# Row normalisation streamed through one core: one hardware DMA queue in a fixed order of load runs and store runs, in place of two queues mixed packet by packet

## The chip, the cores and the metric

The kernel runs on 1 core of one Trainium2 chip. The metric is the device time of one execution in microseconds (us). DVE is the vector engine and ACT the scalar engine, which compute here; SP is the sync engine, which only issues transfers. HBM is the chip's memory, SBUF the buffer in the core. A transfer runs as *packets* on 16 DMA engines. "L" is a load (HBM to SBUF), "S" is a store (SBUF to HBM), and a *turn* is the place in a queue where a load is followed by a store.

## The reference

```python
def reference(x):                      # x: float32 [32, 512, 1024]
    sums = np.sum(np.abs(x), axis=-1, keepdims=True)
    return (x / (sums + 1e-8)).astype(np.float32)
```

67.1 MB are read and 67.1 MB are written, each once; every row of 1024 values is divided by its own sum.

## The kernel before

The 16384 rows are 128 partitions x 128 rows. They are cut into 11 tiles: ten of 12 rows per partition (6 MB each) and one of 8 rows (4 MB), in 4 buffers that take turns. The loads are issued from the sync engine (SP) and the stores from ACT, so they are on two DMA queues.

```python
    R = 12
    BUFS = 4
    ...
    sbuf = ctx.enter_context(tc.tile_pool(name="sbuf", bufs=BUFS))
    ...
    def normalize(x_tile, r0, k, kv):   # DVE: sum of |x|, +eps, 1/x; then
        ...                             # rows 0..kv-1 scaled on DVE, the rest on ACT

    with tc.manual_schedule():
        for i, k in enumerate(rows):
            x_tile = sbuf.tile([P, R, d], FP32)
            nc.sync.dma_start(out=x_tile[:, :k, :], in_=piece(x_flat, i))
            normalize(x_tile, 0, k, k // 2)
            nc.scalar.dma_start(out=piece(out_flat, i), in_=x_tile[:, :k, :])
```

A load into a buffer waits until the store out of that buffer has landed. That wait is on the issuing sequencer (SP), not in the queue.

Of the kernel before, what the change touches and what calls it, by code (L numbers as in the profile page):

```python
# [1 line left out]

# [4 lines left out]

FP32 = mybir.dt.float32
EPS = 1e-8


@with_exitstack
def kernel(
    ctx: ExitStack,
    tc: tile.TileContext,
    x: bass.AP,
    out: bass.AP,
):
    nc = tc.nc
    P = nc.NUM_PARTITIONS  # L20

    x_flat = x.flatten_outer_dims()
    out_flat = out.flatten_outer_dims()
    n, d = x_flat.shape


    R = 12
    BUFS = 4
    per_partition = n // P
    assert n % P == 0  # L30
    rows = [R] * (per_partition // R)
    if per_partition % R:
        rows.append(per_partition % R)

    def piece(flat, i):
        a, k = P * sum(rows[:i]), rows[i]
        return flat[a : a + P * k, :].rearrange("(p r) d -> p r d", p=P)

    sbuf = ctx.enter_context(tc.tile_pool(name="sbuf", bufs=BUFS))
    stats = ctx.enter_context(tc.tile_pool(name="stats", bufs=4))  # L40

    def normalize(x_tile, r0, k, kv):

        s = stats.tile([P, R], FP32)
        nc.vector.tensor_reduce(  # L45
            out=s[:, :k],
            in_=x_tile[:, r0 : r0 + k, :],
            axis=mybir.AxisListType.X,
            op=mybir.AluOpType.add,
            apply_absolute_value=True,  # L50
        )
        nc.vector.tensor_scalar_add(out=s[:, :k], in0=s[:, :k], scalar1=EPS)  # L52
        inv = stats.tile([P, R], FP32)
        nc.vector.reciprocal(out=inv[:, :k], in_=s[:, :k])  # L54
        nc.vector.tensor_mul(  # L55
            out=x_tile[:, r0 : r0 + kv, :],
            in0=x_tile[:, r0 : r0 + kv, :],
            in1=inv[:, :kv].unsqueeze(2).to_broadcast([P, kv, d]),
        )
        for r in range(kv, k):  # L60
            row = x_tile[:, r0 + r, :]
            nc.scalar.activation(  # L62
                out=row,
                in_=row,
                func=mybir.ActivationFunctionType.Copy,
                scale=inv[:, r : r + 1],
            )

    with tc.manual_schedule():
        for i, k in enumerate(rows):  # L70
            x_tile = sbuf.tile([P, R, d], FP32)
            nc.sync.dma_start(out=x_tile[:, :k, :], in_=piece(x_flat, i))  # L72
            normalize(x_tile, 0, k, k // 2)
            nc.scalar.dma_start(out=piece(out_flat, i), in_=x_tile[:, :k, :])  # L74


# [1 line left out]
_INS = ['x']  # L78
_OUTS = [((32, 512, 1024), 'float32')]


# [23 lines left out]
```

## Time and profile before

| | before |
|---|---|
| median of 4 runs | 317.66 us (317.55 to 318.85) |
| span of the profiled run | 315.8 us |
| DVE, ACT busy | 67%, 22% |
| packets on the 16 DMA engines | 98.9% of the span |

Lines of the profile page of the kernel before. The rows of digits are busy tenths in 40 equal slices of the span. The last two lines give packets, MB and the share of the 16 DMA engines' span for each queue.

```profile
span 315.8 us, 227 instructions
DVE 212.4 (67%) x44; ACT 69.0 (22%) x65; POOL 0.2 (0%) x4
DVE  0069999998499079719944991797099449949300
ACT  0010804308007000700440070007003400701300
DMA  8999999999999999999999999999999999999996
GB/s 311 467 417 411 467 367 442 405 454 430 417 448 430 423 461 423 436 442 417 442 442 411 449 436 411 448 436 423 448 430 436 442 413 450 421 448 417 448 403 278
q1 hardware_dynamic: 1584, 67.11, 49.8%
q10 hardware_dynamic: 1584, 67.11, 49.1%
```

The DMA row stands at 9 from the second slice to the last but one, and the two queues (q1 loads, q10 stores) together hold 98.9% of the engines' time. DVE has gaps in every period. So the DMA engines are the limit, and a change can help only by moving the same bytes faster or by shortening the two ends.

Stretches of the same execution, from the windows view: a load-only stretch, two periods of mixed loads and stores, and the store-only end. The last two columns are the DMA share and GB/s.

```profile
core 0: us, DVE busy (x) ACT busy (x) POOL busy (x), PEclk, DMA share, GB/s
20.00:38.00 18.00, 17.90 (x4) 6.19 (x6) 0.00 (x0) 1.00 1.01 437
103.00:132.00 29.00, 19.91 (x5) 6.34 (x7) 0.00 (x0) 1.00 1.00 434
132.00:161.00 29.00, 19.90 (x5) 6.34 (x7) 0.00 (x0) 1.00 1.00 434
285.00:300.00 15.00, 9.92 (x4) 4.27 (x4) 0.00 (x0) 1.00 1.03 446
```

Packets are large (48 KB, 1.8 us), so a stretch of 15 or 18 us can catch a wave of packet starts more or less; the 29 us stretches are one full period and exact. The packet records say it more finely: a 48 KB packet takes 1.815 us in all three stages. 16 x 49152 B / 1.815 us = 433.3 GB/s. This is close to the 435 GB/s that the Trainium skill gives as the ceiling of the 16 ports ("DMA: Bandwidth & Descriptors", section "Where 436 GB/s comes from").

What SP waited for, from the waits view of the DMA queues' own engine (us in total, times, longest):

```profile
SPq L72 <- DMA out_dram<-x_tile: 226.5, 7, 55.2
SPq L72 <- DMA x_tile<-in_x_dram: 15.4, 1, 15.4
```

The seven later loads wait for stores to land; this wait costs nothing as long as the queues still hold work.

### The profile page before, as it was taken

To read this page: it belongs to the slowest core of one execution; us is meant where nothing else is said; L and a number is where in the kernel's file an instruction comes from. 1 tells how busy PE (TensorE), PEld (TensorE's weight loads), DVE (VectorE), ACT (ScalarE), POOL (GpSimd) and SP (SyncE) were. 2 spreads that over 40 slices of the span, in tenths; PEclk is the share of its full clock that TensorE was granted. 3 is DMA by queue.
4 is the path that set the end of the run, shared out by engine and by line. 5 is a ranking of instruction groups with operands and counts; after the bars stand their busy time and mean duration, and the time that the engine had idled before them with its cause. 6 is when DMAs were issued, how large, how long until landed. Compare 5 with 4: busy or idle time off the path is not lost.

```text
span 315.8 us, 227 instructions
## 1 busy us (share of the span) xinstructions
DVE 212.4 (67%) x44; ACT 69.0 (22%) x65; POOL 0.2 (0%) x4
## 2 busy tenths in 40 slices
DVE  0069999998499079719944991797099449949300
ACT  0010804308007000700440070007003400701300
POOL 0000000000000000000000000000000000000000
DMA  8999999999999999999999999999999999999996
GB/s 311 467 417 411 467 367 442 405 454 430 417 448 430 423 461 423 436 442 417 442 442 411 449 436 411 448 436 423 448 430 436 442 413 450 421 448 417 448 403 278
DMA packets 3169, 134.23 MB, mean 425 GB/s; under 512 B 352, under 2 KB 352, under 8 KB 352
## 3 DMA queue, kind: packets, MB, share of 16 engines
q1 hardware_dynamic: 1584, 67.11, 49.8%
q10 hardware_dynamic: 1584, 67.11, 49.1%
q14 instruction: 1, 0.01, 0.0%
HBM read 67.11 MB, written 67.11 MB: 425 GB/s over the span
## 4 chain that ended last, share of the span: by engine, by line
DMA 55%; DVE 25%; another core or an unknown queue 9%; ACT 4%; issue 0%; SPq 0%; DVEq 0%; ACTq 0%
DMA x_tile<-in_x_dram 41%; DVE s L45 19%; DMA out_dram<-x_tile 14%; DVE x_tile L55 6%; ACT x_tile L62 4%; DVE inv L54 0%; DVE s L52 0%; SPq L72 0%; DVEq L54 0%; ACTq L74 0%
## 5 line engine op out<-in xcount | busy, mean ns | idle before, releaser
L45 DVE TENSOR_REDUCE s<-x_tile 128x12 f32<-128x12288 f32 (+1 forms) x11 | 138.2, 12564 | 81.1 <-DMA x_tile<-in_x_dram 81.1
L62 ACT ACTIVATE x_tile<-x_tile,inv 128x1024 f32<-128x1024 f32 x64 | 67.7, 1135 | 207.6 <-DVE inv L54 207.6
L55 DVE TENSOR_TENSOR x_tile<-x_tile,inv 128x6144 f32<-128x6144 f32 (+1 forms) x11 | 70.0, 6364 | 0.4
L62 ACT ACT_TABLE_LOAD x1 | 1.3, 1283 | 18.4 <-DMA x_tile<-in_x_dram 18.4
L54 DVE RECIPROCAL inv<-s 128x12 f32<-128x12 f32 (+1 forms) x11 | 2.5, 226 | 0.9
L52 DVE TENSOR_SCALAR s<-s 128x12 f32<-128x12 f32 (+1 forms) x11 | 1.9, 173 | 0.4
L89 POOL MEMSET const-bfloat16-1.0<- 128x1 bf16 x1 | 0.1, 101 | 0.0
L89 POOL MEMSET const-uint8-127<- 128x1 uint8 x1 | 0.1, 101 | 0.0
L89 POOL MEMSET const-float32-0.0<- 128x1 f32 x1 | 0.1, 98 | 0.2 <-issue 0.2
L89 POOL MEMSET const-float32-1.0<- 128x1 f32 x1 | 0.1, 98 | 0.0
## 6 DMA issues: line engine op xcount, KB each, us to landing
x_tile<-in_x_dram SPq DMA_DIRECT2D x10, 6144.0 KB, 38.5
out_dram<-x_tile ACTq DMA_DIRECT2D x10, 6144.0 KB, 53.5
x_tile<-in_x_dram SPq DMA_DIRECT2D x1, 4096.0 KB, 33.7
out_dram<-x_tile ACTq DMA_DIRECT2D x1, 4096.0 KB, 19.5
```

What stands on the lines that cost most here:

```text
L45: nc.vector.tensor_reduce(out=s[:, :k], in_=x_tile[:, r0 : r0 + k, :], axis=mybir.AxisListType.X, op=mybir.AluOpType.add, apply_absolute_v ...
L52: nc.vector.tensor_scalar_add(out=s[:, :k], in0=s[:, :k], scalar1=EPS)
L54: nc.vector.reciprocal(out=inv[:, :k], in_=s[:, :k])
L55: nc.vector.tensor_mul(out=x_tile[:, r0 : r0 + kv, :], in0=x_tile[:, r0 : r0 + kv, :], in1=inv[:, :kv].unsqueeze(2).to_broadcast([P, kv, d]),)
L62: nc.scalar.activation(out=row, in_=row, func=mybir.ActivationFunctionType.Copy, scale=inv[:, r : r + 1],)
L89: nc = _bacc.Bacc("TRN2", target_bir_lowering=False, num_devices=1)
```

## The change

The intent: take the arbitration away from the hardware. All transfers go into one queue, in a fixed order of longer runs in one direction, so that the engines do not alternate between reading and writing HBM at every packet. Four turns from loads to stores are left (L4 S2, L2 S3, L3 S2, L2 S4).

```diff
+    tiles = {}
+
+    def load(i):
+        k = rows[i]
+        x_tile = sbuf.tile([P, R, d], FP32)
+        tiles[i] = x_tile
+        nc.sync.dma_start(out=x_tile[:, :k, :], in_=piece(x_flat, i))
+        normalize(x_tile, 0, k, k // 2)
+
+    def store(i):
+        nc.sync.dma_start(out=piece(out_flat, i), in_=tiles[i][:, : rows[i], :])
+
+    runs = [("L", 4), ("S", 2), ("L", 2), ("S", 3), ("L", 3), ("S", 2), ("L", 2), ("S", 4)]
     # (two asserts on the totals cut)
     with tc.manual_schedule():
-        for i, k in enumerate(rows):
-            x_tile = sbuf.tile([P, R, d], FP32)
-            nc.sync.dma_start(out=x_tile[:, :k, :], in_=piece(x_flat, i))
-            normalize(x_tile, 0, k, k // 2)
-            nc.scalar.dma_start(out=piece(out_flat, i), in_=x_tile[:, :k, :])
+        done = {"L": 0, "S": 0}
+        for what, m in runs:
+            for _ in range(m):
+                (load if what == "L" else store)(done[what])
+                done[what] += 1
```

More of the change, by code (lines that the diff above doesn't have):

```diff
@@ L67, in normalize @@
             )
-    with tc.manual_schedule():
-        for i, k in enumerate(rows):
-            x_tile = sbuf.tile([P, R, d], FP32)
-            nc.sync.dma_start(out=x_tile[:, :k, :], in_=piece(x_flat, i))
-            normalize(x_tile, 0, k, k // 2)
-            nc.scalar.dma_start(out=piece(out_flat, i), in_=x_tile[:, :k, :])
+    tiles = {}
[8 more added lines that the diff above has]
+    runs = [("L", 4), ("S", 2), ("L", 2), ("S", 3), ("L", 3), ("S", 2), ("L", 2), ("S", 4)]
+    assert sum(m for w, m in runs if w == "L") == len(rows)
+    assert sum(m for w, m in runs if w == "S") == len(rows)
+    with tc.manual_schedule():
+        done = {"L": 0, "S": 0}
[3 more added lines that the diff above has]
+                done[what] += 1
 _INS = ['x']
```

## The prediction

> **What bounds the kernel now.** The DMA engines, from 2 us after the start to the end. On the profile page the row of DMA busy tenths stands at 9 in every slice but the first and last, while DVE is busy 67% and ACT 22%. The queue part gives 49.8% + 49.1% = 98.9% of the 16 engines' span to packets. The windows view shows 434 GB/s in each 29 us period from 103 to 248 us. In the packet records a 48 KB packet takes 1.815 us, load or store, in the load-only stage (5 to 38 us), the mixed stage and the store-only stage (from 282 us). 16 x 49152 B / 1.815 us = 433.3 GB/s, so 134.2 MB need 309.8 us whatever their order. This agrees with the Trainium skill, "DMA: Bandwidth & Descriptors", section "Where 436 GB/s comes from", which puts the ceiling of the 16 ports at 435.2 GB/s.
>
> The span of 315.8 us is then: 1.7 us until the first packet; 309.8 us of packets; about 2.2 us per engine of packets stretched beyond 1.815 us (0.9 us on the first loads, 1.15 us between 38.6 and 44 us, when the first store joins the loads); about 2 us of end (engines finishing up to 1.7 us apart, closing barrier).
>
> **What the change does.** It removes no byte and no DVE or ACT work; it moves 11 store issues (0.34 us each) from ACT to SP and fixes the order. The skill (same page, "Queues, rings and completion order") says an engine alternates between its queues packet by packet. The trace agrees (loads and stores share the mixed stage about equally), and this mixing costs nothing there: two tiles' packets take 29.0 us, 16 x 1.815 = 29.04. So longer runs have no turnaround loss to win back.
>
> **Is there a new bubble?** I walked the order with 14.5 us per 6 MB tile and 19.95 us of DVE per tile. Each load waits for its buffer's store, with at least one whole transfer queued behind that store. The thinnest places are load 4 (issued about 76.5 us, queue full until 90) and load 9 (about 221, full until 235): 13 us of margin. The last compute ends near 283.5 us; its store's turn comes near 303. So the queue never runs empty and DVE stays off the critical path.
>
> **Sum.** Only the stretch at switches can differ. If the 1.15 us at 38 us belongs to a second queue starting, it goes: 316.6. If to the first store, it stays: 317.7. If each of the four load-to-store switches costs as much, 3.4 us come on top: 321. I predict 317.4 us, range 316.0 to 320.3; within 2%: 0.93, faster 0.02, slower 0.05.
>
> **What would show each step right or wrong.** Queue part: one queue with about 99%. Windows view: 433 GB/s in pure-load and pure-store stretches alike; 450 in one would refute the fixed rate. DMA tenths at 9 throughout; a dip near 76, 90, 135, 221 or 236 us would be a bubble or a switch cost. DVE's waits move (idle about 98 to 106 and 146 to 178 us) without lengthening the span. SP's waits are on stores' landings.
>
> **What would make it wrong.** A drain of the queue at each of the 7 changes of direction (over 0.9 us each would be needed to pass 2%); a limit on outstanding transfers of one queue (four loads were accepted at once before); landings reported much later than the data, eating the 13 us margin.

## The result, and the profile after

| | before | after |
|---|---|---|
| median | 317.66 us (317.55 to 318.85, 4 runs) | 318.75 us (318.47 to 318.82, 4 runs) |
| ratio to before, 95% interval | | 1.0024 (1.0000 to 1.0049) |
| span of the profiled run | 315.8 us | 317.1 us |

A ratio is the mean time of one kernel's fast runs over the mean time of the other's fast runs of the same rounds, so it is not quite the ratio of the medians quoted beside it (here the one run of 318.85 lifts the mean of before). By the 2% rule the two are the same. All outputs are right. A repetition with more runs, told below, gave 1.0045 (1.0033 to 1.0057): the changed kernel is slower, by about half a per cent or less.

The same lines of the page, after:

```profile
span 317.1 us, 213 instructions
DVE 212.0 (67%) x44; ACT 69.0 (22%) x65; POOL 0.2 (0%) x4
DVE  0069999999993599995000399999992099991000
ACT  0010804308043008025000006107052003431000
DMA  8999999999999999999999999999999999999995
GB/s 316 465 409 440 446 403 477 347 453 403 465 422 409 471 409 428 465 397 471 422 397 477 415 428 465 397 409 472 409 434 446 401 444 459 415 422 465 415 417 223
q1 hardware_dynamic: 3168, 134.22, 98.5%
```

There is one queue now, and it holds 98.5%. The DMA row is again 9 throughout: no bubble. The DVE row has changed its pattern (three longer gaps), but its sum has not.

Pure-load stretches (20 to 56, 94 to 118, 168 to 203, 242 to 257 us) and pure-store stretches (64 to 90, 124 to 160, 212 to 236, 266 to 305 us) of the changed kernel, from the windows view:

```profile
20.00:56.00 36.00, 35.79 (x8) 10.60 (x11) 0.00 (x0) 1.00 1.01 436
64.00:90.00 26.00, 25.90 (x5) 6.34 (x6) 0.00 (x0) 1.00 0.99 427
94.00:118.00 24.00, 15.31 (x2) 3.94 (x4) 0.00 (x0) 1.00 1.03 446
124.00:160.00 36.00, 22.75 (x5) 9.06 (x9) 0.00 (x0) 1.00 1.00 434
168.00:203.00 35.00, 22.92 (x5) 6.34 (x6) 0.00 (x0) 1.00 1.01 437
212.00:236.00 24.00, 23.66 (x8) 8.92 (x9) 0.00 (x0) 1.00 1.00 435
242.00:257.00 15.00, 3.98 (x1) 0.00 (x0) 0.00 (x0) 1.00 0.97 419
266.00:305.00 39.00, 20.36 (x7) 10.61 (x10) 0.00 (x0) 1.00 0.99 431
```

The view gives 419 to 446 GB/s. It counts a packet whole where it begins, so packets fall in or out at the edges of a stretch: one wave of 16 packets is 0.79 MB, which is 33 GB/s in 24 us. If the bytes of each packet are spread evenly over its time, the packet records give 433.5 to 434.0 GB/s in all eight stretches, and the median 48 KB packet takes 1.815 us in loads and stores alike. The mixed periods before moved 434. There was no cost of alternating that longer runs could win back.

SP's waits after, and two of the DVE waits (sum |x| of a tile, with the idle time ahead of it in brackets), from the waits view and the timeline:

```profile
SPq L79 <- DVE x_tile L55: 168.9, 8, 35.6
SPq L75 <- DMA out_dram<-x_tile: 108.3, 7, 23.6
```

```profile
106.84 12.95 DVE L45 TENSOR_REDUCE s<-x_tile 128x12 f32<-128x12288 f32 x1 [8.69 <-DMA x_tile<-in_x_dram]
...
179.91 12.96 DVE L45 TENSOR_REDUCE s<-x_tile 128x12 f32<-128x12288 f32 x1 [32.98 <-DMA x_tile<-in_x_dram]
```

SP, which now issues the stores too, waits for compute as well as for landings. DVE idles from 98.2 to 106.8 us and from 146.9 to 179.9 us. None of it reaches the end: the last store is issued at 286.7 us and its packets have their turn only from 303 us on.

So where do the 1.3 us of span come from? Each transfer runs on 16 DMA engines, and each engine writes one semaphore record when its share has landed, so the packet records give 16 landing times per transfer. This table is worked out from them: the spread between the first and the last of the 16, in the order of the queue.

```
changed kernel, 16 landings of each transfer: last minus first, us
L 1.1  L 1.1  L 1.1  L 1.6 | S 1.6  S 1.6
L 1.6  L 2.1 | S 2.1  S 2.1  S 2.1
L 2.1  L 2.1  L 2.6 | S 2.6  S 2.6
L 2.6  L 2.8 | S 2.8  S 2.8  S 2.8  S 2.8
kernel before, its last three stores: 1.4  1.4  1.4
```

The spread grows at the last load ahead of each turn, and nowhere else. At the end the first engine is done at 312.94 us (before: 312.83), the last at 315.71 us (before: 314.24). The fast engines lose 0.1 us; the slowest loses 1.5 us, and the kernel ends with the slowest.

The packet durations agree. Time beyond 1.815 us (1.213 us for the last tile's 32 KB packets), as a mean per engine: 0.74 us on the first loads (before 0.96), 1.09 us at the first turn (before 1.16, when the first store joins the loads), and 0.57 us at the later turns (before 0.07 in all the rest of the run). Of these 0.57 us, 0.40 fall on the third turn, where every engine lost something (0.14 to 0.74 us, followed engine by engine as explained below); at the second and fourth turns only three or four engines lost more than 0.1 us.

### The profile page after: what moved, and what is told of

Read it like the earlier page. It is cut to its first block, busy times and chain, and to the rows that moved or that the text cites. A ratio compares the mean times of both kernels' runs of the same rounds, so it can differ in the third digit from the quotient of the medians.

```text
span 317.1 us, 213 instructions
## 1 busy us (share of the span) xinstructions
DVE 212.0 (67%) x44; ACT 69.0 (22%) x65; POOL 0.2 (0%) x4
## 3 DMA queue, kind: packets, MB, share of 16 engines
q1 hardware_dynamic: 3168, 134.22, 98.5%
## 4 chain that ended last, share of the span: by engine, by line
DMA 53%; DVE 29%; another core or an unknown queue 7%; issue 0%; SPq 0%; DVEq 0%
DMA x_tile<-in_x_dram 28%; DMA out_dram<-x_tile 24%; DVE s L45 19%; DVE x_tile L55 10%; DVE inv L54 0%; DVE s L52 0%; SPq L79 0%; SPq L75 0%; DVEq L54 0%
```

## The experiments

The theories that the runs were to tell apart:

- **T1**: each turn on the single queue stretches load packets just ahead of it, most on engines that are already late; the number of turns sets the cost.
- **T2**: engines drift apart by chance, whatever the order.
- **T3**: the cost belongs to having one queue, whatever its order.
- **T4**, a sharper T1: an engine loses because it is late, still loading when the others begin to store; its rival **T5**: certain engines are slow at turns, late or not.

All times with their ratio to the kernel before on the same chip and in the same rounds, and when the first and the last engine finished in the profiled run:

| run | queues, turns | median us (range, runs) | ratio (95% interval) | first / last engine done, us |
|---|---|---|---|---|
| before | 2, mixed | 317.66 (317.55 to 318.85, 4) | | 312.83 / 314.24 |
| after | 1, 4 | 318.75 (318.47 to 318.82, 4) | 1.0024 (1.0000 to 1.0049) | 312.94 / 315.71 |
| after_again | 1, 4 | 319.05 (318.56 to 319.29, 5) | 1.0045 (1.0033 to 1.0057) | 312.85 / 316.25 |
| turns8 | 1, 8 | 320.20 (319.21 to 321.04, 6) | 1.0081 (1.0066 to 1.0095) | 312.75 / 317.26 |
| bubble7 | 1, 8, empties 7 times | 350.38 (349.91 to 350.77, 4) | 1.1032 (1.1018 to 1.1046) | 347.12 / 347.70 |
| early_store | 2, mixed | 317.04 (316.71 to 317.83, 6) | 0.9989 (0.9976 to 1.0001) | 312.94 / 313.91 |
| early_again | 2, mixed | 317.83 (316.81 to 318.14, 6) | 0.9998 (0.9978 to 1.0017) | 312.79 / 315.05 |
| small_runs | 1, 4 | 318.08 (316.98 to 318.55, 6) | 1.0013 (0.9998 to 1.0027) | 312.78 / 314.64 |
| lag4_runs | 1, 4 | 320.17 (319.93 to 320.39, 4) | 1.0082 (1.0069 to 1.0095) | 313.44 / 317.25 |
| lag4_two | 2, mixed | 322.38 (321.21 to 324.41, 6) | 1.0154 (1.0129 to 1.0179) | 313.32 / 321.43 |
| lag12_runs | 1, 4 | 319.52 (318.89 to 320.78, 6) | 1.0049 (1.0028 to 1.0070) | 314.34 / 317.78 |
| r4_two | 2, mixed | 318.29 (318.16 to 318.33, 5) | 1.0020 (1.0008 to 1.0032) | 314.38 / 315.33 |
| r4_runs | 1, 4 | 319.80 (319.32 to 320.26, 6) | 1.0068 (1.0055 to 1.0081) | 314.40 / 316.81 |
| r4_alt | 1, 21 | 320.59 (320.42 to 321.31, 5) | 1.0098 (1.0083 to 1.0113) | 314.28 / 317.42 |

### The changed kernel again, unedited

> The changed kernel once more, unedited, for its own spread. T1: again stretched packets only at the turns from loads to stores, about 1 us per engine at the first and 0.05 to 0.5 us at the later ones, ends 2.3 to 3.2 us apart, 318.4 to 318.9 us. T2: the stretches move to other places and the ends can be 1.4 us apart, with a time near 317.6 us in some runs.

Measured: 319.05 us. The spread of landings, again in the order of the queue: 1.4, 1.5, 1.5, 2.2 at the first turn, 2.6 at the second, 2.6 at the third, 3.4 at the fourth. Packets stretched 1.2 us per engine at the first turn, 0.26 us later. So in these two profiles the places repeat (the last loads ahead of turns), the amounts do not: the third turn, which cost 0.5 us of spread in the first profile, cost nothing here, and the fourth cost 0.8 in place of 0.2. The median is 0.15 us above what I had expected at most. This answers T2 in part: the amounts vary from run to run, the places hardly.

### Eight turns in place of four

```diff
-    runs = [("L", 4), ("S", 2), ("L", 2), ("S", 3), ("L", 3), ("S", 2), ("L", 2), ("S", 4)]
+    runs = [("L", 4), ("S", 2)] + [("L", 1), ("S", 1)] * 6 + [("L", 1), ("S", 3)]
```

> The changed kernel with the same single queue, the same tiles and no bubble, but with 8 turns from loads to stores in place of 4: four loads, two stores, then six times one load and one store, one load, three stores. Theory T1 (each turn stretches the last load packets before it, the trailing engine most; the three later turns of the changed kernel put its last engine about 1.4 us later): four more turns cost 1.2 to 2.4 us, so 319.9 to 321.2 us, and the 16 engines end 3.5 to 5 us apart in place of 2.8. Theory T2 (the drift of the engines is chance of the run) and T3 (the cost comes from having one queue, whatever its order): the same as the changed kernel, 318.4 to 319.0 us, ends 1.4 to 2.8 us apart.

Measured: 320.20 us, as T1 had it. The two intervals to the kernel before, 1.0081 (from 1.0066) and the repeated changed kernel's 1.0045 (to 1.0057), do not overlap, and both kernels ran on one chip. One queue and the same bytes, more turns, more time: neither T3 nor T2 can be the whole story. (A part that belongs to the single queue as such is not excluded: no run mixes loads and stores finely in one queue without turns.) The page shows no bubble that could have done it instead (DMA row and queue of this run):

```profile
DMA  8999999999999999999999999999999999999993
q1 hardware_dynamic: 3168, 134.22, 98.1%
```

The landings show how:

```
eight turns, 16 landings of each transfer: last minus first, us
L 1.2  L 1.2  L 1.2  L 1.6 | S 1.6  S 1.6
L 2.1 | S 2.1    L 2.9 | S 2.9    L 3.0 | S 3.0
L 3.4 | S 3.4    L 4.1 | S 4.1    L 4.1 | S 4.1
L 4.5 | S 4.5  S 4.5  S 4.5
```

Every increase is at a load directly ahead of a store, none at a store. Following single engines through their packets (possible here because the 16 sequences keep their order in time) shows more: after the first turn twelve engines lost nothing worth telling (at most 0.12 us in one packet; one of them also lost 0.3 us to a packet of another queue, see the smaller tiles), and four lost 0.1 to 0.8 us at a time, nearly always in the eighth, which is the last, packet of a load. While those last packets ran, on average 7 to 14 of the other engines were already storing; two small losses earlier in a load (0.1 and 0.2 us) came while at most one was.

### One store pending in place of two: the queue runs empty

```diff
-    runs = [("L", 4), ("S", 2), ("L", 2), ("S", 3), ("L", 3), ("S", 2), ("L", 2), ("S", 4)]
+    runs = [("L", 4)] + [("S", 1), ("L", 1)] * 7 + [("S", 4)]
```

> The changed kernel with one store pending in place of two: four loads, then seven times one store and one load, then four stores. Each of the seven loads now waits for the landing of the store directly ahead of it, with nothing queued behind that store. My walk of the order says that the queue empties seven times, each for about 2 to 2.5 us (0.5 us from the last byte to the sequencer, about 1 to 1.8 us from issue to the first packet, plus the spread of the engines): 332 to 337 us, and seven dips in the DMA row. If a rival is right that the order hardly matters because the queue hides it, it stays at 318 to 320 us.

Measured: 350.38 us; my estimate was too low by 13 us or more. The dips are there, seven of them (slices 9, 13, 17, 21, 25, 29, 33 of the DMA row; then SP's waits):

```profile
DMA  9999999969996999689979996999799969998997
q1 hardware_dynamic: 3168, 134.22, 93.5%
```

```profile
SPq L75 <- DMA out_dram<-x_tile: 237.5, 7, 39.2
```

Each of the seven costs more than the idle time. From the packet records, per engine and per dip: 2.8 us idle (I had estimated 2 to 2.5), 0.8 us of slow packets when loads restart, as at the very start of the kernel, and 1.25 us of stretched packets at the turn that follows, on all engines, as at the first turn. The sum is 4.85 us; seven times that is 34 us, and the span is 33.3 us longer than before. The last two terms were missing from my walk. This is also the measure of what the change got right: with two stores pending in place of one, a load still waits for a landing, but always with another transfer behind it. The Trainium skill has the reason ("DMA: Bandwidth & Descriptors", "Anatomy of one DMA — SWDGE (gpsimd) path"; the section is about transfers issued another way, but this sentence speaks of the DMA engines): the engines do not wait on semaphores, the issuing sequencer does, before it issues. The trace agrees: the fifth load was issued at 78.3 us, 0.3 us after the last landing of the first store (78.0 us) and not before.

One more thing is seen here: the engines end only 0.6 us apart. During the run the spread of landings goes up and down between 0.6 and 2.2 us, without the steady growth of the eight-turn run.

### A small first tile, two queues

```diff
-    rows = [R] * (per_partition // R)
-    if per_partition % R:
-        rows.append(per_partition % R)
+    rows = [2] + [R] * 10 + [6]
```

> The kernel before (two queues) with tiles of 2, ten times 12 and 6 rows, so that a small store is issued at about 9.5 us and the next one at about 39 us. If the stretch of about 1.1 us per engine belongs to the first store of the run, it moves to 9 to 13 us and nothing is stretched near 41 us; time as before, 317.3 to 317.9 us. If it belongs to any start of stores on engines that were loading only, it is seen twice, at 9 to 13 us and near 41 us, and the time rises by about 1 us to 318.3 to 318.9 us.

Measured: 317.04 us, ratio 0.9989 (0.9976 to 1.0001). Loads were stretched twice: 0.65 us per engine between 10 and 20 us, around the small first store, and 0.68 us from 42 to 46 us, when stores joined again after the store queue had been idle. So the stretch is not that of the first store of the run alone; it comes when stores set in on engines that were only loading. But the sum (1.33 us) is not much larger than the 1.16 us before, and the time did not rise as that expectation had it. Was the 0.6 us gain real?

> The two-queue kernel with tiles of 2, ten times 12 and 6 rows once more, unedited, to see whether its 0.6 us below the kernel before is real: 316.8 to 317.3 us if it is, 317.4 to 317.8 us if it was chance.

Measured: 317.83 us, ratio 0.9998. The gain was chance. The two stretches were seen again, but unequal: 0.19 us and 0.76 us per engine. In this profile the engines ended 2.3 us apart, in the other, of the same code, 1.0 us. So the drift exists on two queues too, and no run beats the kernel before by more than noise.

### A small first tile, one queue

The same edit of the rows in the changed kernel, with the order L4 S2 L2 S3 L3 S3 L3 S4.

> The changed kernel with tiles of 2, ten times 12 and 6 rows on its single queue (4 loads, 2 stores, 2 loads, 3 stores, 3 loads, 3 stores, 3 loads, 4 stores: four turns as in the changed kernel). In the two-queue kernel such a small first tile left the engines 0.7 us apart after the first tiles in place of 1.1 and removed most of the slow first packets. T4: less initial lateness leaves less to amplify: 317.2 to 318.4 us, ends 1 to 2.3 us apart. If lateness at the start does not matter for what the turns cost: 318.5 to 319.0 us, ends 2.5 to 3.2 us apart.

Measured: 318.08 us, engines 1.9 us apart at the end, from 0.3 us after the first tiles: both within what T4 expected, and below the range of its rival. (The profile is of a run of 317.57 us, one of the faster ones.) The median ratio is 0.13% above the kernel before (0.9998 to 1.0027), against 0.24% (1.0000 to 1.0049) and 0.45% (1.0033 to 1.0057) for the changed kernel. So a small first tile may take back part of what the single queue costs; the intervals of the first pair overlap, and this is not shown. The base, as just told, does not gain from it. The places are less clear here than T4 says: of the growth of the spread after the first turn, nearly half (0.5 of 1.1 us) came in the first of the three loads ahead of the third turn, just behind a run of stores.

### Four engines made late

```diff
     with tc.manual_schedule():
+        extra = lag.tile([P, 768], FP32)
+        nc.sync.dma_start(out=extra[:68, :], in_=x_flat[:68, :768])
```

The extra load is useless on purpose. The trace shows four more semaphore records and 68 packets of 3 KB, so it did run on four engines. On one queue:

> The changed kernel with one small useless load ahead of everything: 68 partitions of 3 KB into a scratch tile nobody reads. Only 4 of the 16 DMA engines should carry it (4 semaphore records in the trace would show that), 17 packets each, 52 KB or about 1.9 us. So four chosen engines start their real work about 1.9 us late. Theory T4 (a turn from loads to stores costs only the engines that are still loading when the others begin to store): these four land late from the first tile on and lose another 0.3 to 0.7 us at each of the four turns; ends 3.5 to 5.5 us apart, 320.0 to 322.0 us. Theory T5 (certain fixed engines are slow at turns, late or not): the four keep their 1.9 us and no more, other engines drift by 1.4 us behind the rest as they did in the changed kernel; ends 2 to 3.3 us apart, 318.6 to 319.6 us.

Measured: 320.17 us, as T4 had it. The four landed the first tile 0.4 to 1.6 us after the last of the other twelve, and the last store 1.5 to 3.2 us after it. They lost 0.2 to 0.55 us in the load ahead of the second turn (the latest of them 0.4 more in the load before that), 0.55 to 0.8 us ahead of the third, up to 0.23 us ahead of the fourth. One of them lost 0.4 us more just behind the third turn, where an 8 KB packet of another queue ran; such packets are told of with the smaller tiles below. The other twelve stayed within 0.7 us of each other to the end. So in this run the engines that were late are those that lost; T5 fails, unless by accident I chose the engines that are slow by themselves. A surprise: the first turn, which stretches the engines by about 1 us each in the other one-queue kernels of this tile size, stretched them by 0.06 us here. I have no explanation.

On two queues:

> The same small load ahead of the kernel before (two queues). T4: on two queues every engine mixes loads and stores all the time, so lateness does not grow: the four engines stay 1.5 to 2.2 us behind from the first tile to the last, 318.5 to 319.5 us. If lateness grows on two queues too, T4 is wrong about what the order of runs does: over 320 us.

Measured: 322.38 us. This was a plain miss, and it refutes the second half of T4. On two mixed queues lateness grows too, even faster: the last engine ended 8.1 us after the first. The landings show the late engines losing 0.2 to 1.9 us in nearly every 29 us period while the others mostly keep 29.0 us. So long runs are not needed for the loss. In the profile of the undisturbed kernel before, most engines alternate nearly in step (in the mixed stage, four loads in five ran beside fewer than 6 storing engines), and nobody loses. That being out of step is the cause is argued from these two profiles and not shown: one engine of the kernel before was out of step and lost nothing (see the end).

### Twelve engines made late

The extra load with 108 partitions of 4 KB in place of 68 of 3 KB, on one queue.

> As the run with four late engines on one queue, but the useless load ahead has 108 partitions of 4 KB and should lie on 12 engines (12 semaphore records), 9 packets and about 1.5 us each: now twelve engines are late and four are early. Theory T4a (an engine loses at a turn when it is late, however many are late with it): the twelve lose another 1.2 to 1.6 us over the later turns, as the four did; 319.8 to 321.0 us. Theory T4b (only a minority loses: the last loads of few engines under the stores of many): the twelve lose nothing at the later turns, the early four neither; time rises by the extra load alone, 318.3 to 319.6 us, and the ends stay as far apart as the first landings.

Measured: 319.52 us, which lies in the range of T4b, but the run does not decide. The extra load ran on twelve engines (12 semaphore records), yet the lateness was gone when the first tile landed: all 16 landed within 0.4 us. What the profile (of the slowest of the six runs, 320.78 us) shows instead: from this nearly perfect start one engine lost time in five loads, 0.5 and 0.25 us in the two ahead of the second turn, 0.4 and 0.8 us in the first and third ahead of the third turn, 1.1 us in the last one ahead of the fourth, and ended 3.4 us after the first engine. A good start does not protect. Here some of the stretched packets stood at the beginning of a load run, so the last packet ahead of a turn is the usual place, not the only one.

### Smaller tiles, to count turns

`R = 4` and `BUFS = 12` in place of 12 and 4: 32 tiles of 2 MB, packets of 16 KB. Three orders: two queues mixed; one queue in long runs (L12 S6 L6 S9 L9 S6 L5 S11); one queue alternating (L12 S4, nineteen times L1 S1, L1 S9).

> The kernel before (two queues, mixed) with 32 tiles of 4 rows in 12 buffers in place of 11 tiles of up to 12 rows in 4 buffers: the same bytes in packets of 16 KB. If the packets run at the same rate: 317 to 319 us, engines' ends 0.7 to 1.6 us apart. It is the base for the two runs that follow.

> The same 32 tiles of 4 rows on one queue in long runs with four turns from loads to stores: 12 loads, 6 stores, 6 loads, 9 stores, 9 loads, 6 stores, 5 loads, 11 stores. T4: like the changed kernel against the kernel before, 0.5 to 2 us above the mixed two queues; ends 2 to 3.5 us apart.

> The same 32 tiles on one queue with 21 turns: 12 loads, 4 stores, then nineteen times one load and one store, one load, 9 stores. T4: 17 more turns at 0.2 to 0.6 us each for the late engines, so 3 to 9 us above the long runs, 322 to 328 us, ends 5 to 12 us apart. If late engines stop losing once they lag by a whole run of 4.8 us: about 322 to 323 us. If the number of turns does not matter (T2, T3): within 0.7 us of the long runs.

Measured: 318.29, 319.80 and 320.59 us. The first engine ends at the same time in all three (314.4, 314.4, 314.3 us); the last at 315.3, 316.8 and 317.4 us. One queue in long runs costs 1.5 us over two, like the change itself (1.1 and 1.4 us by the medians). The alternating order costs 0.8 us more, and here I missed: 17 more turns were to cost 3 us at least. The landings of the alternating order say why:

```
alternating order, tiles of 4 rows: last minus first landing, us, by number of the transfer (even numbers from 16 on are loads)
15: 0.5  16: 0.5  18: 0.9  20: 1.2  22: 1.5  24: 2.3  26: 2.3  28: 2.6  30: 3.1  32: 3.1  34: 3.1  ...  63: 3.1
```

The spread grows only at loads that stand ahead of a store, as before; then it stops at 3.1 us and does not move for the last twelve turns. So in this run a turn has no fixed price: the three latest engines lost time at turns up to a point and then no more.

The small tiles also show something else that makes an engine late. The page of the long runs lists a third queue:

```profile
q14 instruction: 3, 0.02, 0.0%
```

These three packets of 8 KB ran at 105.2, 178.2 and 233.5 us, each for 0.31 us, and each in a gap of 0.30 to 0.32 us in the packets of just one engine. Those engines lost 1.0, 0.65 and 0.6 us there or in the next packets, and they are the three that ended last (2.4, 1.0 and 1.5 us after the first; the other 13 within 0.6 us). The one that ended last lost 1.3 us more ahead of the third and fourth turns. So in this profile a part of the lateness began with these packets and not at a turn. They are not enough alone: the two-queue run had two of them, and its engines ended 0.95 us apart. In the alternating order three of the five latest engines had such a packet too. In the one-queue runs with 48 KB packets that never ran empty there are one or two of them, and the engine that ended last was never one that met them: in the changed kernel the one at 217.6 us met an engine that ended 0.6 us after the first.

## Why the prediction was right

- **The limit** (DMA engines at 433 GB/s in any order): shown. Pure loads and pure stores after ran at 433.5 to 434.0 GB/s and mixed periods before at 434, and the first engine was done within 0.2 us of the same moment before, after, repeated and with eight turns (312.75 to 312.94 us).
- **Longer runs win nothing back**: shown, by the same numbers. The skill's statement that an engine alternates between its queues packet by packet ("DMA: Bandwidth & Descriptors", "Queues, rings and completion order") agrees with this trace: in the mixed stage of the kernel before (103 to 248 us), 1096 packets can be matched to the one packet that ended as they began, and 979 of these pairs change queue. The alternating was free here. So was having two issuing engines; the same page ("Issuing engines are not separate DMA queues") says that it only saves issue time.
- **No bubble**: right, and the margin was real. I had load 4 issued at about 76.5 us with the queue full until 90; it was issued at 77.9 us, and the transfer behind the store landed from 90.4 us on. Load 9: said 221 and 235, measured 224.0 and 235.6. Where the margin was taken away on purpose, the time rose by 10%.
- **DVE off the path**: right. It idles where the prediction said (98 to 106, 146 to 178 us), and once more before 253 us.
- **The stretch at switches** was the only open term, and it is the one that was mis-sized. My centre of 317.4 us let part of the 1.15 us go. It stayed whole (1.09 us, and 1.2 us in the repetition), and the later turns added a little. Above all I had put it as an equal loss on all engines. In fact the mean engine lost 0.26 to 0.57 us at the later turns, but the last engine lost 1.4 to 2 us more than the first against the kernel before, and the last engine sets the time. The measured 318.75 us lies 1.35 us above the centre, inside the range. That is partly luck: the range had been widened toward a loss of all engines at every turn (321 us), and the term that did grow, the end (engines up to 1.7 us apart), had been taken as unchanged; it measured 2.8 us (before: 1.4).

What stays open: why a late engine's last load packet is stretched. That it happens mostly beside the stores of others is seen, but this alone is not enough: in the alternating order with small tiles the three latest engines stop losing while the stores of others go on, and in the kernel before one engine loaded for the whole mixed stage beside about 10 storing engines and lost nothing. Open, too, are why the first turn costs all engines about 1 us with 48 KB packets (0.1 us with 16 KB), why it cost little in the two runs with four late engines (0.06 and 0.26 us), and whether the engines that fall behind are always the same (the records do not name them).

## What to carry to other kernels

When the packets already fill all DMA engines at one rate in both directions, do not expect the order or the number of queues to make them faster (no order did here); look at what the first and the last engine do instead, because the kernel ends with the last. If you fix an order in one queue, keep at least one whole transfer issued behind every landing that a later load waits for: losing that cost 4.7 us each time here. Leave the mixing to the two queues unless you have a reason not to; the fixed order cost 0.2 to 0.5%.

## What the Trainium skill lacked or had wrong

- "DMA: Bandwidth & Descriptors", "Where 436 GB/s comes from", says that for transfers between HBM and SBUF the HBM side, about 358 GB/s, binds. The sentence lacks its condition, which the same page gives just above it ("Measured"): that is the share when both cores of a pair stream. With one core at work it did not bind: 433.9 GB/s over a 29 us period of loads and stores mixed (12.58 MB), 433.5 to 434.0 in pure runs.
- The same page has no account of the 16 engines drifting apart over a kernel (it calls two of them usually slower, with a guess that ties this to transfers issued from gpsimd, which this kernel has none of). Here they ended 0.95 to 2.3 us apart on two undisturbed queues and 1.9 to 4.5 us apart on one undisturbed queue that never ran empty, and this was nearly the whole difference in time.
- No page tells the cost of a turn from loads to stores: 1.0 to 1.2 us per engine at the first turn with 48 KB packets (0.06 in one run; 0.1 with 16 KB packets), then mostly 0 for engines on time and 0.1 to 1.1 us for late ones; at one turn of the changed kernel every engine lost 0.1 to 0.7 us. Behind turns from stores to loads a single engine lost up to 0.6 us in a few places; most lost nothing.
- The same page gives a fixed cost of about 2 us per DMA, fitted to transfers issued from gpsimd. For a queue of SP that runs empty between transfers of 6 MB the runs show 4.7 us of time each (32.8 us over seven). By the packet records 2.8 us are idle engines, 0.8 us slow packets at the restart and 1.25 us stretched packets at the turn that follows.
